# The last two row tiles of a hybrid decoder block: last tile summed in two column halves, preceding tile scaled half on GpSimd, tail in program order

## The chip, the cores and the metric

One core of a Trainium2 chip runs the whole program. The time is device microseconds of that core; it is the median of several executions. The profile is one execution recorded by the hardware profiler; its times count from the start of its span.

## The reference, cut to what matters

The program computes one decoder block on 1024 tokens of width 1024: attention and spatial gating side by side, a gated MLP with a convolution, and a final RMSNorm. The change lies in the last matrix product and in that final norm:

```python
h = h + conv_ffn(rmsnorm(h, norm_ffn_g[layer]), w_up[layer], conv_w[layer],
                 conv_b[layer], w_down[layer])
...
return rmsnorm(h, norm_final_g)        # h * rsqrt(mean(h*h) + 1e-6) * gain, row by row

def conv_ffn(x, w_up, conv_w, conv_b, w_down):
    ...
    return (jax.nn.silu(g) * a) @ w_down
```

A row of the output can be scaled only when the sum of squares over all 1024 columns of that row is known, so the norm of a row tile begins when the last part of that tile's product has been added.

## The kernel before, in words

The output is worked on in eight row tiles of 128 tokens, y0 to y7, each 128 x 1024 in SBUF. The product with `w_down` is done by Strassen's scheme (Winograd's form), in 512-wide column halves `lo` (0 to 511) and `hi` (512 to 1023): seven block products named A11, S4, A12, S1, S2, S3 and A22, each of which is computed by `dprod` for four row tiles. Each matmul with full precision is made of three float32r matmuls (high times high, high times low, low times high). The contraction runs over NP = 11 pairs of blocks, so a row tile of a block product takes 33 matmuls into one PSUM bank.

The last product is A22. Its first eight contraction steps (line 1703) go over the four row tiles in turn; the last three, the `rest`, are prepared first and then finished one row tile at a time (lines 1707 to 1710), so that bank 4 is complete first (for y4), then bank 5 (y5), 6 (y6) and 7 (y7). Nine matmuls of 512 columns lie between one tile's completion and the next. These four banks are the PSUM tiles named `s`; the other four are named `b`.

When a bank of A22 is complete, this is done for its row tile (lines 1803 to 1806 and `finish`, 1766 to 1783). By then the `hi` half is complete and already multiplied by the gain, and its squares are summed.

1. DVE subtracts the bank from the `lo` half (L1804).
2. ACT squares the `lo` half and sums the squares (L1805: an ACTIVATE and an ACTIVATION_READ_ACCUMULATOR), then takes the square root (L1770), where the other half's mean square comes in as the bias `ssb`.
3. DVE takes the reciprocal (L1771).
4. ACT scales the `hi` half (L1775) while DVE scales the `lo` half by reciprocal and gain (L1776, SCALAR_TENSOR_TENSOR).
5. SyncE's queue (SP) issues the store of the whole tile, 512 KB (L1783). For y7 step 4 runs in two pieces of 256 columns, the two `lo` quarters are stored from SP (L1779) and the `hi` half from ACT's own queue (L1781).

The order of instructions on each engine isn't the order in which they are written. The class `Pace` records all instructions of the program; `settle` works out dependences, gives each instruction a due time from the due times of those that need it, and then `run` lets a model of the engines pick, for each engine, whichever recorded instruction can start first, and of those the one due first. Two regions of the DRAM tensor `out` are compared there by their first and last address alone, so two column ranges of the same rows count as overlapping and the model lets the second store begin only when the first has landed. The order so found is fixed for each engine. Between stores to different columns the built program has no such wait: it waits only for what produces the data, and for the earlier user of the same completion semaphore, of which there are eight in rotation.

Of the kernel before, what the change touches and what calls it, by code (L numbers as in the profile page):

```python
# [11 lines left out]
AF = mybir.ActivationFunctionType  # L12
# [20 lines left out]
class Pace:  # L33
# [77 lines left out]
    def start(self):  # L111
        self.first = len(self.tc.nc.cur_bb.bb.instructions)

    def view(self, a):

        ap = getattr(a, "bass_ap", None)
        t = getattr(ap, "tensor", None)
        if t is None:
            return None
        dims = [tuple(d) for d in a.ap]  # L120
        if t.name in self.slot:
            if self.slot[t.name][0].space == "psum":
                return t.name, 0, P, 1, True
            step = 1
            for s in t.shape[1:]:
                step *= s
            p0, off = divmod(ap.offset, step)
            n = dims[0][1] if dims[0][0] else 1
            mask, run = 1, 1
            starts = [off]  # L130
            rest = sorted((d for d in dims[1:] if d[0]), reverse=True)
            if rest and rest[-1][0] == 1:
                run = rest.pop()[1]
            for s, c in rest:
                starts = [o + s * k for o in starts for k in range(c)]
            mask = 0
            for o in starts:
                mask |= ((1 << run) - 1) << o
            return t.name, p0, p0 + n, mask, True
        end = ap.offset + sum(abs(s) * (c - 1) for s, c in dims)  # L140
        return t.name, ap.offset, end + 1, 1, False
# [57 lines left out]
    def settle(self, rounds=3):  # L199

        names = {mybir.EngineType.PE: "PE", mybir.EngineType.DVE: "DVE", mybir.EngineType.Activation: "ACT",
                 mybir.EngineType.Pool: "POOL", mybir.EngineType.SP: "SP"}
        ops, seen, uses, opens = [], {}, {}, {}
        for i in list(self.tc.nc.cur_bb.bb.instructions)[self.first:]:
            eng = names.get(i.engine)
            rd = [v for v in map(self.view, i.ins) if v]
            wr = [v for v in map(self.view, i.outs) if v]
            if eng is None or not wr:
                continue
            k = len(ops)  # L210
            if eng == "PE" and not i.start_tensor_calc:
                rd = rd + wr
            deps = set()
            for w, vs in ((False, rd), (True, wr)):
                for name, a, b, m, tile_ in vs:
                    old, keep, hits = seen.setdefault(name, []), [], 0
                    for o in old:
                        hit = o[2] < b and a < o[3] and o[4] & m
                        if hit and (w or o[1] or self.bank(name) and ops[o[0]][1] != eng):
                            deps.add(o[0])  # L220
                            hits += 1
                        if not (w and hit and a <= o[2] and o[3] <= b and not o[4] & ~m and tile_):
                            keep.append(o)
                    keep.append((k, w, a, b, m))
                    seen[name] = keep
                    if tile_:
                        uses.setdefault(name, set()).add(k)
                        if not hits:
                            opens.setdefault(name, set()).add(k)
            deps.discard(k)  # L230
            c = self.cost(i, eng)
            ops.append((i, eng, c, deps, SET.get(str(getattr(i, "func", "")).split(".")[-1], 0) if eng == "ACT" else 0))
        prev = self.prior(uses)
        for name, ks in opens.items():
            for old in prev[name]:
                for k in ks:
                    ops[k][3].update(uses[old] - {k})
        whose = {}
        for name, ks in uses.items():
            whose.setdefault(self.slot[name][0], set()).update(ks)  # L240
        for p in {p: 0 for p, _ in self.slot.values()}:
            if p.after:
                ops.append((None, "TURN", (0, 0, 0), set().union(*(whose[q] for q in p.after)), 0))
                for k in whose[p]:
                    ops[k][3].add(len(ops) - 1)
        n = len(ops)
        succ = [[] for _ in range(n)]
        for k, o in enumerate(ops):
            for d in o[3]:
                succ[d].append(k)  # L250
        line, count = [k for k in range(n) if not ops[k][3]], [len(o[3]) for o in ops]
        for k in line:
            for q in succ[k]:
                count[q] -= 1
                if not count[q]:
                    line.append(q)
        assert len(line) == n, [(ops[k][0].name, str(ops[k][0])) for k in range(n) if count[k]][:4]
        at, t = [0.0] * n, 0.0
        for k, o in enumerate(ops):
            at[k] = t  # L260
            if o[1] == "PE":
                t += o[2][0]
        best = None
        for _ in range(rounds):
            due = [0.0] * n
            for k in reversed(line):
                o = ops[k]
                d = at[k] if o[1] == "PE" else at[k] + SLACK
                for s in succ[k]:
                    d = min(d, due[s] - (o[2][0] if ops[s][1] == o[1] != "SP" else o[2][1] + HOP))  # L270
                due[k] = d
            order, start, end = self.run(ops, succ, due)
            if best is None or end < best[0]:
                best = (end, order)
            at = start
        for eng, seq in best[1].items():
            for x, y in zip(seq, seq[1:]):
                self.tc.add_manual_dep(ops[y][0], ops[x][0].name, mybir.DependencyInfo(
                    mybir.DependencyClass.NoSync, mybir.DependencyReason.DATA), reason="order")
        return best[0]  # L280
# [63 lines left out]
def block_kernel(ctx: ExitStack, tc: tile.TileContext, xT, xtok, wuv, wv, wqk, wf, cpk, xg, bfv,  # L344
# [1338 lines left out]
    def dprod(xn_, wsrc, bk, first, wb=None, tail=1):  # L1683

        def prep(p_):
            xr = dt_("xr", [P, 512], F32)
            sp.dma_start(out=xr, in_=hx[p_, XI[xn_]])
            if wb is not None:
                wload(p_, wb)
            xh = dt_("xh", [P, 2, 512], F32R)  # L1690
            split_w(xr, (xh[:, 0], xh[:, 1]))
            src = wsrc(p_)
            wh = dt_("wh", [P, 2, 512], F32R)
            split_w(src, (wh[:, 0], wh[:, 1]))
            return xh, wh

        def step(m, p_, xh, wh):
            ms = slice(m * P, (m + 1) * P)
            for n, (xi, wi) in enumerate(((0, 0), (0, 1), (1, 0))):
                pe.matmul(banks[bk + m], xh[:, xi, ms], wh[:, wi, :], start=(first and p_ == 0 and n == 0),  # L1700
                          stop=(p_ == NP - 1 and n == 2), skip_group_check=True)

        for p_ in range(NP - tail):
            xh, wh = prep(p_)
            for m in range(4):
                step(m, p_, xh, wh)
        rest = [(p_, *prep(p_)) for p_ in range(NP - tail, NP)]
        for m in range(4):
            for r in rest:
                step(m, *r)  # L1710
# [55 lines left out]
    def finish(tt, done):  # L1766
# [6 lines left out]
        for c in range(0, 512, n):  # L1773
            d, t = slice(done.start + c, done.start + c + n), slice(todo.start + c, todo.start + c + n)
            act.activation(y[tt][:, d], y[tt][:, d], AF.Copy, scale=r)  # L1775
            dve.scalar_tensor_tensor(out=y[tt][:, t], in0=y[tt][:, t], scalar=r, in1=gfb[:, t],  # L1776
                                     op0=ALU.mult, op1=ALU.mult)
            if tt == 7:
                sp.dma_start(out=out[tt * P:(tt + 1) * P, t], in_=y[tt][:, t])  # L1779
        if tt == 7:  # L1780
            act.dma_start(out=out[tt * P:(tt + 1) * P, done], in_=y[tt][:, done])  # L1781
        else:
            sp.dma_start(out=out[tt * P:(tt + 1) * P, :], in_=y[tt])  # L1783

    def gain(tt, half):
        dve.tensor_tensor(out=y[tt][:, half], in0=y[tt][:, half], in1=gfb[:, half], op=ALU.mult)
# [9 lines left out]
    for m in range(4):  # L1796
# [2 lines left out]
        act.activation(x3[m], y[4 + m][:, hi], AF.Square, accum_out=ssf[:, 4 + m, 1:2])  # L1799
        first_half(4 + m, 1)  # L1800
        gain(4 + m, hi)
    dprod("A22", t4, 4, False, tail=3)
    for m in range(4):
        dve.tensor_tensor(out=y[4 + m][:, lo], in0=y[4 + m][:, lo], in1=banks[4 + m], op=ALU.subtract)  # L1804
        act.activation(x3[m], y[4 + m][:, lo], AF.Square, accum_out=ssf[:, 4 + m, 0:1])  # L1805
        finish(4 + m, hi)
    pace.settle()
    dn.release()
    upl.release()
# [47 lines left out]
```

## Time and profile before

| what | value |
|---|---|
| time, median of 3 runs | 1056.11 us (1056.04 to 1056.29) |
| time of the profiled execution | 1056.11 us |
| its span, first to last instruction | 1054.4 us |
| PE busy | 1045.7 us (99% of the span) |
| DVE busy | 914.1 us (87%) |
| ACT busy | 578.6 us (55%) |
| POOL (GpSimd) busy | 251.4 us (24%) |
| granted TensorE clock, mean | 0.999 |

The profiled execution took as long as the median run, 1.7 us more than its span; that difference lies outside the span. A row of the timeline gives start, length, engine, line, operation, output and inputs, and how many instructions are merged into it. Starts on one engine can lie closer than the lengths, since an instruction begins while the one before it still drains. A row of the table of stretches gives, for each engine, the busy time in the stretch, and at its end the granted clock, the mean busy share of the 16 DMA engines and the GB/s that they moved.

### The profile page before, as it was taken

How to read it: one execution, taken by the hardware profiler on the slowest of the kernel's cores; microseconds unless marked ns; L12 is line 12 of the kernel's file. 1: busy time of each engine (PE TensorE's matmuls, PEld its weight loads, DVE VectorE, ACT ScalarE, POOL GpSimd, SP SyncE). 2: the span in 40 equal slices, each digit the busy share in tenths (PEclk: the TensorE clock that was granted, in tenths of full speed). 3: DMA queues.
4: the chain of work that ended last, by engine and by line, in shares of the span. 5: the costliest groups of instructions: out<-in, count | busy, mean ns of one | idle time of the engine just before them, and what ended most of it. 6: DMA issues, size and time to landing. Idle time of an engine off the chain costs nothing.

```text
span 1054.4 us, 14160 instructions
## 1 busy us (share of the span) xinstructions
PE 1045.7 (99%) x4865; PEld 863.3 (82%) x4865; DVE 914.1 (87%) x1384; ACT 578.6 (55%) x1007; POOL 251.4 (24%) x212
## 2 busy tenths in 40 slices
PE   9999999999999999999999999999999999999997
PEld 6888788888888888888888888888888888888885
DVE  6996998988888869999999899999998895697774
ACT  6668555477777747645444344444444454454653
POOL 0002234233362250073432533424322000000000
PEclk9999999999999999999999999999999999999999
DMA  9243167965664454214323242332423995333352
GB/s 333 91 152 105 53 188 232 293 208 162 205 212 147 140 195 164 80 63 147 108 92 120 102 135 64 115 126 76 130 74 104 349 391 194 95 96 100 91 180 89
DMA packets 65176, 158.22 MB, mean 150 GB/s; under 512 B 7680, under 2 KB 8520, under 8 KB 65104
## 3 DMA queue, kind: packets, MB, share of 16 engines
q1 hardware_dynamic: 64672, 156.50, 45.3%
q10 hardware_dynamic: 432, 0.82, 0.3%
q8 instruction: 38, 0.62, 0.2%
q14 instruction: 34, 0.28, 0.1%
HBM read 114.98 MB, written 42.31 MB: 149 GB/s over the span
## 4 chain that ended last, share of the span: by engine, by line
PE 98%; DMA 0%; ACT 0%; DVE 0%; SPq 0%; issue 0%; ACTq 0%
PE s L1512 23%; PE b L1512 17%; PE s L1700 11%; PE b L1700 9%; PE s L551 6%; PE b L551 5%; PE fl L1183 4%; PE s L700 4%; PE po L1107 3%; PE b L700 3%; PE tr L1088 3%; PE lg L1068 2%; PE lg L1067 2%; PE b L1423 1%; PE b L1421 1%; PE b L1422 1%
## 5 line engine op out<-in xcount | busy, mean ns | idle before, releaser
L1512 PE MATMUL s<-xT,whb 128*128 128x512 f32 x804 | 189.7, 389 | 0.0
L1512 PEld LDWEIGHTS s<-xT,whb 128*128 128x128 f32 x804 | 150.7, 188 | 31.9 <-DVE whb L450 0.3
L1512 PE MATMUL b<-xB,wha 128*128 128x512 f32 x528 | 126.9, 389 | 0.0
L1700 PE MATMUL s<-whb,wha 128*128 128x512 f32 x528 | 120.2, 389 | 0.0
L1700 PEld LDWEIGHTS s<-whb,wha 128*128 128x128 f32 x528 | 99.1, 188 | 20.6
L1512 PEld LDWEIGHTS b<-xB,wha 128*128 128x128 f32 x528 | 99.0, 188 | 20.5
L444 ACT CAST whb<-sg 128x512 fp32r<-128x512 f32 x82 | 50.8, 621 | 92.9 <-PE s L1512 83.2
L444 ACT CAST wha<-sg 128x512 fp32r<-128x512 f32 x77 | 48.0, 624 | 92.4 <-PE b L1700 43.6
L1700 PE MATMUL b<-whb,wha 128*128 128x512 f32 x396 | 90.2, 389 | 0.0
L450 DVE TENSOR_TENSOR wha<-sg,wha 128x512 fp32r<-128x512 f32 x77 | 53.0, 688 | 40.1 <-ACT wha L444 40.1
L1700 PEld LDWEIGHTS b<-whb,wha 128*128 128x128 f32 x396 | 74.3, 188 | 15.4
L1401 POOL TENSOR_TENSOR sg<-raw,raw 128x512 f32<-128x512 f32 x20 | 37.3, 1864 | 159.9 <-DVE whb L450 159.9
L1512 PE MATMUL s<-xB,whb 128*128 128x512 f32 x264 | 63.5, 389 | 0.0
L1183 PE MATMUL fl<-whl,H 128*128 128x512 f32 x192 | 62.7, 406 | 0.0
L450 DVE TENSOR_TENSOR whb<-sg,whb 128x512 fp32r<-128x512 f32 x82 | 58.5, 732 | 2.5 <-ACT whb L444 2.2
L1512 PE MATMUL b<-xT,whb 128*128 128x512 f32 x252 | 60.7, 389 | 0.0
L1094 ACT CAST pt<-tr 128x512 fp32r<-128x512 f32 (+2 forms) x96 | 45.6, 476 | 24.7 <-PE tr L1088 20.9
L1099 DVE TENSOR_TENSOR pt<-tr,pt 128x512 fp32r<-128x512 f32 (+1 forms) x96 | 52.0, 551 | 7.2 <-ACT pt L1094 6.7
L1512 PEld LDWEIGHTS s<-xB,whb 128*128 128x128 f32 x264 | 49.5, 188 | 10.6 <-DVE h L1583 0.3
L1399 POOL TENSOR_TENSOR sg<-raw 128x512 f32<-128x512 f32 x20 | 41.6, 2081 | 64.5 <-DMA raw<-wup 61.3
L1512 PEld LDWEIGHTS b<-xT,whb 128*128 128x128 f32 x252 | 47.3, 188 | 9.8
L1107 PE MATMUL po<-pt,V 128*128 128x512 f32 (+1 forms) x192 | 48.5, 347 | 0.0
(373 smaller groups left out, 2287.2 us busy)
## 6 DMA issues: line engine op xcount, KB each, us to landing
raw<-wup SPq DMA_DIRECT2D x44, 512.0 KB, 3.5
sg<-hx SPq DMA_DIRECT2D x77, 256.0 KB, 2.6
hx<-hs SPq DMA_DIRECT2D x44, 256.0 KB, 4.0
hx<-ca SPq DMA_DIRECT2D x33, 256.0 KB, 2.3
xT<-wdn SPq DMA_DIRECT2D x28, 256.0 KB, 5.4
raw<-wqk SPq DMA_DIRECT2D x8, 512.0 KB, 3.7
kd<-G SPq DMA_DIRECT2D x16, 256.0 KB, 5.9
qd<-G SPq DMA_DIRECT2D x16, 256.0 KB, 3.6
```

The costliest lines, as they stand in the source:

```text
L444: act.copy(h, src)
L450: return eng.tensor_tensor(out=l, in0=src, in1=f32(h), op=ALU.subtract)
L551: pe.matmul(banks[m], xs(n, xi, k)[:, ms], w[:, wi, :], start=(first and k == 0 and c == 0), stop=(k == 3 and c == 2), skip_group_check=True)
L700: pe.matmul(ps, w[:, wi, ks], xs(n, xi, k), start=(first and c == 0), stop=(c == 11), skip_group_check=True)
L1094: act.copy(pt[:, 0, o:512], ps[:, o:512])
L1099: dve.tensor_tensor(out=pt[:, 1, o:512], in0=ps[:, o:512], in1=f32(pt[:, 0, o:512]), op=ALU.subtract)
L1107: pe.matmul(self.po[hf][:, o:512], lhs, pt[:, s, o:512], start=(k == 0 and s == 0), stop=(k == 4 * hf + 3 and s == 1), skip_group_check=True)
L1183: pe.matmul(self.bank, sgT[k][:, xi, ts_], self.w[hf, k][:, wi, :], start=(k == 0 and i == 0), stop=(k == 3 and i == 2))
L1399: pool.tensor_tensor(out=s[0], in0=a21, in1=a22, op=ALU.add)
L1401: pool.tensor_tensor(out=s[2], in0=a21, in1=a11, op=ALU.add)
L1512: pe.matmul(ps, w[:, wi, ks], xb[:, xi, k, :], start=(first and n == 0), stop=(n == 11), skip_group_check=True)
L1700: pe.matmul(banks[bk + m], xh[:, xi, ms], wh[:, wi, :], start=(first and p_ == 0 and n == 0), stop=(p_ == NP - 1 and n == 2), skip_group_c ...
```

## The change

The tail, from the last three contraction steps of A22 on, is written out instead of being looped, and `settle` is told by `plain()` where it begins: instructions of the tail get due times in the order in which they are written, and they no longer set due times of what comes ahead of them.

- **y7 in two column halves.** The last three contraction steps of y7 run for columns 0 to 255 into bank 7, then for columns 256 to 511 into bank 0 (a `b` tile, idle by then): 18 matmuls of 256 columns instead of 9 of 512. When the first nine are done, DVE subtracts the whole of bank 7 from `lo`, and ACT squares and sums columns 0 to 255. When the second nine are done, DVE subtracts columns 256 to 511 of bank 0, and ACT squares and sums those. In between a new ACT instruction (Identity, one column) adds the first quarter's mean square to `ssb`.
- **y5 and y6 scaled half on GpSimd.** For y5 and y6 GpSimd scales the `hi` half (a tensor_scalar multiply) where ACT did; y4 keeps ACT. The stores of y5 and y6 are split: the `hi` half is stored after GpSimd, the `lo` half after DVE, 256 KB each.
- **y6 behind the last subtraction.** `store(6, pool)` is written behind the last subtraction of y7, so that DVE scales y6's `lo` half after it.

```diff
@@ settle
+            if j >= self.mark:
+                tail.add(k)
...
                 d = at[k] if o[1] == "PE" else at[k] + SLACK
+                if k in tail:
+                    due[k] = 1e9 + k
+                    continue
@@ dprod
-        def step(m, p_, xh, wh):
+        def step(m, p_, xh, wh, cs=slice(0, 512), at=None):
...
-                pe.matmul(banks[bk + m], xh[:, xi, ms], wh[:, wi, :], start=(first and p_ == 0 and n == 0),
+                pe.matmul(banks[bk + m if at is None else at][:, cs], xh[:, xi, ms], wh[:, wi, cs],
+                          start=((first and p_ == 0 or at == 0 and p_ == NP - tail) and n == 0),
...
+        if tail > 1:
+            return lambda m, cs, at=None: [step(m, *r, cs, at) for r in rest]
@@ tail
-    dprod("A22", t4, 4, False, tail=3)
-    for m in range(4):
-        dve.tensor_tensor(out=y[4 + m][:, lo], in0=y[4 + m][:, lo], in1=banks[4 + m], op=ALU.subtract)
-        act.activation(x3[m], y[4 + m][:, lo], AF.Square, accum_out=ssf[:, 4 + m, 0:1])
-        finish(4 + m, hi)
+    last = dprod("A22", t4, 4, False, tail=3)
+    pace.plain()
+    def half_sum(tt, cs):
+        dve.tensor_tensor(out=y[tt][:, lo], in0=y[tt][:, lo], in1=banks[tt], op=ALU.subtract)
+        act.activation(x3[tt - 4][:, cs], y[tt][:, cs], AF.Square, accum_out=ssf[:, tt, tt // 7:tt // 7 + 1])
+    def root(tt):
+        r = ssf[:, tt, 0:1]
+        act.activation(r, r, AF.Sqrt, bias=ssb[:, tt:tt + 1], scale=1.0 / 1024)
+        dve.reciprocal(r, r)
+    def scaled(tt, cs):
+        dve.scalar_tensor_tensor(out=y[tt][:, cs], in0=y[tt][:, cs], scalar=ssf[:, tt, 0:1], in1=gfb[:, cs],
+                                 op0=ALU.mult, op1=ALU.mult)
+    def store(tt, eng):
+        r, rows = ssf[:, tt, 0:1], slice(tt * P, (tt + 1) * P)
+        if eng is act:
+            act.activation(y[tt][:, hi], y[tt][:, hi], AF.Copy, scale=r)
+            scaled(tt, lo)
+            sp.dma_start(out=out[rows, :], in_=y[tt])
+        else:
+            pool.tensor_scalar(out=y[tt][:, hi], in0=y[tt][:, hi], scalar1=r, scalar2=None, op0=ALU.mult)
+            sp.dma_start(out=out[rows, hi], in_=y[tt][:, hi])
+            scaled(tt, lo)
+            sp.dma_start(out=out[rows, lo], in_=y[tt][:, lo])
+    for tt in (4, 5, 6):
+        last(tt - 4, lo)
+        half_sum(tt, lo)
+        root(tt)
+        if tt < 6:
+            store(tt, act if tt == 4 else pool)
+    qs = [slice(c, c + 256) for c in range(0, 1024, 256)]
+    last(3, qs[0])
+    half_sum(7, qs[0])
+    last(3, qs[1], 0)
+    dve.tensor_tensor(out=y[7][:, qs[1]], in0=y[7][:, qs[1]], in1=banks[0][:, qs[1]], op=ALU.subtract)
+    act.activation(ssb[:, 7:8], ssf[:, 7, 1:2], AF.Identity, bias=ssb[:, 7:8], scale=1.0 / 1024)
+    act.activation(x3[3][:, qs[1]], y[7][:, qs[1]], AF.Square, accum_out=ssf[:, 7, 0:1])
+    store(6, pool)
+    root(7)
+    r = ssf[:, 7, 0:1]
+    for c in range(2):
+        act.activation(y[7][:, qs[2 + c]], y[7][:, qs[2 + c]], AF.Copy, scale=r)
+        scaled(7, qs[c])
+        sp.dma_start(out=out[7 * P:8 * P, qs[c]], in_=y[7][:, qs[c]])
+    act.dma_start(out=out[7 * P:8 * P, hi], in_=y[7][:, hi])
```

The end of DVE's order before (`s` are the banks of A22, `gms` holds the sums of squares, `gfb` the gain):

```order
L1771 RECIPROCAL gms_996<-gms_996 128x1
L1776 SCALAR_TENSOR_TENSOR y5_8302<-y5_8302,gms_996,gfb_7809 128x512
L1771 RECIPROCAL gms_996<-gms_996 128x1
L1776 SCALAR_TENSOR_TENSOR y6_8304<-y6_8304,gms_996,gfb_7809 128x512
L1804 TENSOR_TENSOR y7_8306<-y7_8306,s_1357_7817 128x512
L1771 RECIPROCAL gms_996<-gms_996 128x1
L1776 SCALAR_TENSOR_TENSOR y7_8306<-y7_8306,gms_996,gfb_7809 128x256 x2
```

And in the changed kernel (`b_1350` is bank 0):

```order
L1825 SCALAR_TENSOR_TENSOR y5_8302<-y5_8302,gms_996,gfb_7809 128x512
L1814 TENSOR_TENSOR y7_8306<-y7_8306,s_1357_7817 128x512
L1821 RECIPROCAL gms_996<-gms_996 128x1
L1851 TENSOR_TENSOR y7_8306<-y7_8306,b_1350_7810 128x256
L1825 SCALAR_TENSOR_TENSOR y6_8304<-y6_8304,gms_996,gfb_7809 128x512
L1821 RECIPROCAL gms_996<-gms_996 128x1
L1825 SCALAR_TENSOR_TENSOR y7_8306<-y7_8306,gms_996,gfb_7809 128x256 x2
```

The subtraction of y7 has become two, and the scaling of y6 moved from ahead of it to behind both.

The end of SyncE's queue before:

```order
L1687 DMA sg_1593_9517<-hx_116 128x512
L1783 DMA out<-y4_8300 128x1024
L1783 DMA out<-y5_8302 128x1024
L1783 DMA out<-y6_8304 128x1024
L1779 DMA out<-y7_8306 128x256 x2
```

And in the changed kernel, where L1837 stores a `hi` half, L1839 a `lo` half and L1860 a quarter of y7:

```order
L1834 DMA out<-y4_8300 128x1024
L1837 DMA out<-y5_8302 128x512
L1837 DMA out<-y6_8304 128x512
L1860 DMA out<-y7_8306 128x256
L1839 DMA out<-y5_8302 128x512
L1839 DMA out<-y6_8304 128x512
L1860 DMA out<-y7_8306 128x256
```

The `lo` halves of y5 and y6 stand behind the first quarter of y7, and the second quarter of y7 behind them. On ACT's queue the store of y7's `hi` half stays last. Ahead of the tail one pair of rows changes places: DVE splits the weights of the ninth contraction step (`whb_9505`) after two gain multiplications instead of before them.

More of the change, by code (lines that the diff above doesn't have):

```diff
@@ L112, in start, with plain @@
         self.first = len(self.tc.nc.cur_bb.bb.instructions)
+    def plain(self):
+        self.mark = len(self.tc.nc.cur_bb.bb.instructions)
     def view(self, a):
@@ L203, in settle @@
         ops, seen, uses, opens = [], {}, {}, {}
-        for i in list(self.tc.nc.cur_bb.bb.instructions)[self.first:]:
+        tail = set()
+        for j, i in list(enumerate(self.tc.nc.cur_bb.bb.instructions))[self.first:]:
             eng = names.get(i.engine)
@@ L1777, in finish @@
                                      op0=ALU.mult, op1=ALU.mult)
[L1778 to L1783, printed above, removed]
+        sp.dma_start(out=out[tt * P:(tt + 1) * P, :], in_=y[tt])
     def gain(tt, half):
```

## The prediction

> **What bounds the kernel now.** I read the page's chain first, to see where a change can pay at all.
>
> ```profile
> span 1054.4 us, 14160 instructions
> PE 98%; DMA 0%; ACT 0%; DVE 0%; SPq 0%; issue 0%; ACTq 0%
> ```
>
> TensorE carries the chain for 98% of the span, and the change leaves TensorE's work alone except for its last nine matmuls. So everything is decided in the last microseconds. Second, the chain piece by piece over those (start, length, what), and the timeline for TensorE's last stretch and the last stores:
>
> ```profile
> 1034.82 10.44 PE s L1700 x46
> ...
> 1045.28 0.70 DVE y L1804
> ...
> 1046.00 0.73 ACT xB L1805 x2
> ...
> 1046.76 0.30 ACT gms L1770
> ...
> 1047.09 0.17 DVE gms L1771
> ...
> 1047.29 0.75 DVE y L1776
> 1048.04 0.61 DVE y L1804
> ...
> 1048.67 0.73 ACT xB L1805 x2
> ...
> 1049.43 0.30 ACT gms L1770
> ...
> 1049.76 0.18 DVE gms L1771
> ...
> 1049.95 0.91 ACT y L1775 x2
> ```
>
> ```profile
> 1039.19 8.10 PE L1700 MATMUL s<-whb,wha 128*128 128x512 f32 x35
> 1050.47 0.83 SPq L1779 DMA_DIRECT2D out<-y  x2
> 1050.89 0.40 ACTq L1781 DMA_DIRECT2D out<-y  x1
> ```
>
> TensorE ends at 1039.19 + 8.10 = 1047.29, but the chain leaves it at 1045.26, when y6's bank is complete: y6 goes through subtraction, squares, root, reciprocal and its scaling on DVE (1047.29), and only then does DVE subtract y7's bank (pipelined start 1047.96). y7 thus waits 0.67 us for DVE. Then squares, root, reciprocal, scaling, and the stores are issued between 1050.47 and 1051.30. The remaining 3.1 us to 1054.40 are transfers and their end. Third, therefore, the stretches (last two numbers: busy share of the DMA engines, GB/s), with the issue of y4's store for the delay between issue and data:
>
> ```profile
> 1044.04 0.34 SPq L1783 DMA_DIRECT2D out<-y  x1
> ```
>
> ```profile
> 1044.40:1044.80 0.40, 0.40 (x3) 0.35 (x2) 0.16 (x1) 0.21 (x1) 0.00 (x0) 1.00 0.00 0
> 1044.80:1045.20 0.40, 0.40 (x3) 0.32 (x3) 0.00 (x0) 0.40 (x2) 0.00 (x0) 1.00 0.85 338
> 1048.40:1051.20 2.80, 0.00 (x0) 0.00 (x0) 1.29 (x4) 1.92 (x5) 0.00 (x0) 1.00 0.95 375
> 1051.20:1051.60 0.40, 0.00 (x0) 0.00 (x0) 0.00 (x0) 0.00 (x0) 0.00 (x0) 0.80 0.67 218
> 1051.60:1052.80 1.20, 0.00 (x0) 0.00 (x0) 0.00 (x0) 0.00 (x0) 0.00 (x0) 0.50 0.95 335
> 1052.80:1053.20 0.40, 0.00 (x0) 0.00 (x0) 0.00 (x0) 0.00 (x0) 0.00 (x0) 0.50 0.28 87
> 1053.20:1054.40 1.20, 0.00 (x0) 0.00 (x0) 0.00 (x0) 0.00 (x0) 0.00 (x0) 0.50 0.00 0
> ```
>
> Data begin about 0.82 us after an issue starts (0.85 of the second stretch is busy, so from 1044.86). The stretch to 1051.20 moves 2.80 x 375 = 1,050 KB, which is y5 and y6; the three behind it move 87 + 402 + 35 = 524 KB, which is y7. The last byte leaves at 1052.8 + 35/335 = 1052.90, and 1.50 us later the span ends. The transfer engines are 95% busy in both large stretches: the tail has a second limit, bytes, hard behind the chain.
>
> **The change, part by part.** Rows for the pieces, before the sums:
>
> ```profile
> 1045.89 0.15 DVE L1771 RECIPROCAL gms<-gms 128x1 f32<-128x1 f32 x1
> 1046.08 0.75 DVE L1776 SCALAR_TENSOR_TENSOR y<-y,gms,gfb 128x512 f32<-128x512 f32 x1
> 1046.76 0.29 ACT L1770 ACTIVATE gms<-gms 128x1 f32<-128x1 f32 x1
> 1046.96 1.32 ACT L1775 ACTIVATE y<-y,gms 128x512 f32<-128x512 f32 x2
> L1099 DVE TENSOR_TENSOR pt<-tr,pt 128x256 fp32r<-128x256 f32 x16 | 6.7, 416 | 0.0
> L1094 ACT CAST pt<-tr 128x256 fp32r<-128x256 f32 x16 | 5.8, 365 | 4.2 <-PE lg L1067 2.5 <-PE tr L1088 1.0 <-PE lg L1068 0.6
> L1775 ACT ACTIVATE y<-y,gms 128x256 f32<-128x256 f32 x2 | 0.9, 500 | 0.2 <-DVE gms L1771 0.2
> ```
>
> *TensorE.* 18 matmuls of 256 columns replace 9 of 512. 512 columns are (8.10 - 0.39) / 34 = 0.227 us apart. No row has 256 in a series; 384 columns are 0.18 apart, and four of 128 columns, each with weights of its own, (0.60 - 0.27) / 3 = 0.11:
>
> ```profile
> 228.20 0.34 PE L1067 MATMUL lg<-x 128*128 128x384 f32 x1
> 228.38 0.34 PE L1068 MATMUL lg<-x,x 128*128 128x384 f32 x1
> 230.45 0.60 PE L1088 MATMUL tr<-ident,G 128*128 128x128 f32 x4
> ```
>
> So 256 lie between 0.11 and 0.18; following the step from 512 to 384 I take 0.13: 18 x 0.13 = 2.34 against 9 x 0.227 = 2.04, 0.3 us more. Halves are complete near 1046.35 and 1047.5.
>
> *DVE.* y5's scaling starts at 1046.08 as before, the next instruction 0.67 later. y7's first subtraction takes that place at 1046.75 (its data have been ready for 0.4 us), y6's reciprocal follows 0.61 later at 1047.36, the second subtraction 0.19 behind that at 1047.55 (TensorE is ready at 1047.5), and by L1099's 0.42 us it ends at 1047.97. Before, the only subtraction ended near 1048.65. y6's scaling then runs until about 1048.65, under ACT's work.
>
> *ACT.* y7's first squares (256 columns; 0.365 to 0.50, I take 0.42) and their sum run from 1047.45 to 1047.97, and the new Identity starts at 1048.0. The next instruction can start 0.20 later, as L1775 does behind L1770, so Identity costs 0.2 us: second squares at 1048.20. They and their sum take 0.73 - 0.21 = 0.52; the root begins at 1048.75, the reciprocal at 1049.08 and the scaling at 1049.27 instead of 1049.95. **The chain to the scaling is 0.68 us shorter**: 0.67 of DVE's wait and 0.21 of the squares gained, 0.2 lost again. No table load stands in the tail of ACT's order, before or after, so none is counted.
>
> *The stores.* y7's first quarter can be issued at 1050.47 - 0.68 = 1049.79 and the `hi` half from ACT at 1050.21. But on SP's queue two stores that were ready long before, the `lo` halves of y5 (done 1046.8) and y6 (1048.7), now stand behind that first quarter, and SP issues in order. At 0.34 us each they go out at 1050.13 and 1050.47, and the last quarter at 1050.81, against 1050.90 before: of 0.68 us the last issue keeps 0.1. And the bytes behind the first quarter have doubled: 1,049 KB (512 KB of y7, 256 KB each of y5 and y6) against 524.
>
> First data at 1049.79 + 0.82 = 1050.61. The first 0.4 us carry one small store alone, 87 KB as in the row at 1051.20. 962 KB are left, at 335 GB/s (y7's short rows) to 375 (whole tiles): 2.57 to 2.87 us, so the last byte leaves at 1053.58 to 1053.88, I take 1053.7, against 1052.90. If the first 0.4 us are full too it is 1053.4. **Sum: 0.8 us later**, with bounds +0.5 and +1.0.
>
> *GpSimd.* Its multiplies are of a kind that no row shows.
>
> ```profile
> L1139 POOL CAST A<-t 128x512 fp32r<-128x512 f32 x4 | 2.5, 614 | 0.2
> 260.02 0.61 POOL L1139 CAST A<-t 128x512 fp32r<-128x512 f32 x1
> L1399 POOL TENSOR_TENSOR sg<-raw 128x512 f32<-128x512 f32 x20 | 41.6, 2081 | 64.5 <-DMA raw<-wup 61.3 <-DVE whb L450 2.5 <-ACT whb L444 0.7
> 798.58 1.29 POOL L1402 TENSOR_TENSOR sg<-sg,raw 128x512 f32<-128x512 f32 x1 [2.50 <-DVE whb L450]
> ```
>
> Bounds are 0.61 (a copy) and 2.08 (two inputs beside a busy DVE); nearest is the copy, one tensor in and one out, and I take 0.7. y5's runs from 1046.1, y6's from 1047.55 to 1048.25; both stores are issued before 1048.7 and their bytes are through by 1050.3. Cover ends at 1049.79, when y7's first quarter wants the queue. The copies that leave ACT (1.32 us) weren't on the chain.
>
> *DVE's weights* for the ninth step now come about 1.4 us later than here:
>
> ```profile
> 1026.91 0.69 DVE L450 TENSOR_TENSOR whb<-xT,whb 128x512 fp32r<-128x512 f32 x1
> ```
>
> TensorE first needs them at 1039.19, so this costs nothing.
>
> **The forecast** is 1056.11 (the profiled execution, which equals the median) + 0.8 = 1056.9 us. Changes within 0.2%, 2.1 us, count as no change here.
>
> **Rivals.**
>
> *The bytes don't queue* and the last issue sets the end: 1050.81 against 1050.90, so 0.1 us is gained, 1056.0; if the early halves slip through beside y7 and only ACT's last store counts, 0.68, 1055.4. For it: SP has idle time between 1048.7 and 1049.8, and the transfers are spread over 16 engines. Against it: a busy share of 0.95 with only half these bytes. The Trainium skill ("DMA: Bandwidth & Descriptors", section "Anatomy of one DMA — SWDGE (gpsimd) path") fits each DMA as a fixed 2.0 us and bytes over 436 GB/s; taken alone, the last 128 KB would land 2.3 us after issue, and the end would move with that issue, as in this rival. The rows of this trace bear a slower rate and a queue out.
>
> *GpSimd is late and holds SP's queue* (slower). Its two multiplies stand ahead of y7's first quarter on SP. From 1046.1, they decide when together they pass 3.7 us (1049.79). At 2.08 each y6's `hi` half goes out at 1050.3 and joins the burst: from 1051.0, 1,311 KB at 355 GB/s end at 1054.7, +1.8, 1057.9; each further us adds one, so beyond 4.5 us together it is slower by over 0.2%. For it: L1399's mean, and GpSimd idle since 799.9. Against it: this kernel's first copy on GpSimd (260.02) took 0.61 like the later ones. The Trainium skill ("GPSIMD Engine Reference", section "2.1 Instruction dispatch") says that the first call of a freshly loaded kernel pays about 6 us more; the end would then be near 1061. No run here shows such a first call.
>
> *TensorE's halves cost 0.18 each*: 3.24 us for 18, the second half complete at 1048.4 instead of 1047.5. DVE then waits for it and scales y6 later; the chain's 0.68 is gone, and the doubled burst ends 1.5 to 1.7 us later than before: 1057.7. Against it: a half must cost less than 384 columns.
>
> **How the numbers follow.** Forecast 0.70 (1056.5 to 1057.2), bytes that don't queue 0.16 (1055.4 to 1056.3), GpSimd late 0.10 (1057.5 up), slow halves 0.04 (1057.7). The range from 1055.5 to 1058.0 takes in the first two and the lower part of the others, with room for unsharp terms. Faster by over 0.2% would need 2.1 us where the chain yields 0.68: 0.03. Slower by over 0.2% is the upper half of the late GpSimd and a rest: 0.07. Within 0.2%: 0.90.
>
> **What would show it.** Right: the subtraction of y7 starts near 1046.75, y7's scaling near 1049.3, four issues on SP follow each other from 1049.8 without a pause, and the DMA engines stay over 90% busy from 1051 to 1053.6. Wrong: a GpSimd multiply over 1.7 us, SP's first quarter of y7 issued after 1050.2, idle stretches between the last transfers, or a last byte before 1053.0.

## The result and the profile after

| what | before | changed |
|---|---|---|
| time, median of 22 runs each | 1056.22 us (1055.78 to 1057.35) | 1058.16 us (1056.90 to 1059.32) |
| ratio, 95% interval | | 1.0018 (1.0012 to 1.0024) |
| profiled execution, its span | 1056.11, 1054.4 us | 1058.28, 1056.5 us |

The change costs 1.94 us. That lies within the 0.2% called no change (the interval reaches just beyond it), but it is more than twice the 0.8 us that the prediction summed, and the time lies outside its range (1055.5 to 1058.0). Nearest to it is the rival with the late GpSimd, 1057.9 us.

The page of the changed kernel (its head, and GpSimd's group of the tail: busy time, mean ns of one, idle time ahead of it), and then the chain piece by piece (start, length, what), show TensorE at 98% as before, and a shorter way from y6's bank to y7's scaling.

```profile
span 1056.5 us, 14186 instructions
PE 98%; DMA 1%; ACT 0%; DVE 0%; SPq 0%; issue 0%; ACTq 0%
...
L1836 POOL TENSOR_SCALAR y<-y,gms 128x512 f32<-128x512 f32 x2 | 3.9, 1956 | 246.1 <-DVE gms L1821 246.1
```

```profile
1034.95 10.67 PE s L1709 x47
...
1045.65 0.69 DVE y L1814
...
1046.44 0.75 DVE y L1825
1047.19 0.61 DVE y L1814
...
1049.62 0.91 ACT y L1858 x2
```

The tails of profiles must be laid on each other at a common point, for they don't start alike: over the kernels told of here, the subtraction of y4, ahead of everything that differs, starts between 1040.87 and 1042.77 us after the span's start, 1041.20 before the change. Here it starts at 1041.57. From there to y7's scaling it is 1049.62 - 1041.57 = 8.05 us, against 1049.95 - 1041.20 = 8.75: the chain is 0.70 us shorter. To the end of the span it is 14.93 us against 13.20: 1.73 longer. (The medians differ by 1.94; a single profile doesn't tell 0.2 us from chance.) So 2.4 us were lost behind the scaling. The timeline of the changed kernel, engine by engine, shows where:

```profile
1041.57 0.69 DVE L1814 TENSOR_TENSOR y<-y,s 128x512 f32<-128x512 f32 x1 [3.41 <-PE s L1709]
...
1046.52 1.24 PE L1709 MATMUL b<-whb,wha 128*128 128x256 f32 x9
...
1046.51 3.90 POOL L1836 TENSOR_SCALAR y<-y,gms 128x512 f32<-128x512 f32 x2 [246.07 <-DVE gms L1821]
...
1050.44 0.33 SPq L1837 DMA_DIRECT2D out<-y  x1
1050.81 0.43 SPq L1860 DMA_DIRECT2D out<-y  x1
1051.29 1.29 SPq L1839 DMA_DIRECT2D out<-y  x2
1052.68 0.54 SPq L1860 DMA_DIRECT2D out<-y  x1
...
1050.55 0.41 ACTq L1861 DMA_DIRECT2D out<-y  x1
```

GpSimd's two multiplies take 3.90 us together, to 1050.41. Only then can SP issue y6's `hi` half (1050.44), and behind it y7's first quarter (1050.81). That is the 1,956 ns for one in the page's row, and SP's waits for it (total, times, longest) say the same:

```profile
SPq L1837 <- POOL y L1836: 5.3, 2, 3.9
```

Last, the stretches (granted clock, busy share of the DMA engines and GB/s at the end of each row):

```profile
1050.40:1051.20 0.80, 0.00 (x0) 0.00 (x0) 0.10 (x1) 0.12 (x1) 0.01 (x1) 0.50 0.00 0
1051.20:1054.80 3.60, 0.00 (x0) 0.00 (x0) 0.00 (x0) 0.00 (x0) 0.00 (x0) 0.50 1.00 362
1054.80:1056.40 1.60, 0.00 (x0) 0.00 (x0) 0.00 (x0) 0.00 (x0) 0.00 (x0) 0.50 0.02 5
```

For 0.8 us nothing is transferred, and then everything is left: 3.60 x 362 + 1.60 x 5 = 1,311 KB, that is y7 (524), the `lo` halves of y5 and y6 (524) and y6's `hi` half (262). The engines are full (share 1.00) until the last byte at about 1054.83, which is 13.26 us behind y4's subtraction, against 1052.90 - 1041.20 = 11.70 before.

### The profile page after: what moved, and what is told of

It is laid out like the page before. It is cut to its first block, busy times and chain, and to the rows that moved or that the text cites. A ratio compares the mean times of both kernels' runs of the same rounds, so it can differ in the third digit from the quotient of the medians.

```text
span 1056.5 us, 14186 instructions
## 1 busy us (share of the span) xinstructions
PE 1046.0 (99%) x4874; PEld 864.3 (82%) x4874; DVE 915.1 (87%) x1385; ACT 576.7 (55%) x1008; POOL 254.1 (24%) x214
## 4 chain that ended last, share of the span: by engine, by line
PE 98%; DMA 1%; ACT 0%; DVE 0%; SPq 0%; issue 0%; ACTq 0%
PE s L1521 23%; PE b L1521 17%; PE s L1709 11%; PE b L1709 8%; PE s L560 6%; PE b L560 5%; PE fl L1192 4%; PE s L709 4%; PE po L1116 3%; PE b L709 3%; PE tr L1097 3%; PE lg L1077 2%; PE lg L1076 2%; PE b L1432 1%; PE b L1430 1%; PE b L1431 1%
## 5 line engine op out<-in xcount | busy, mean ns | idle before, releaser
L1709 PE MATMUL s<-whb,wha 128*128 128x512 f32 (+1 forms) x528 | 119.2, 387 | 0.0
L1709 PE MATMUL b<-whb,wha 128*128 128x512 f32 (+1 forms) x405 | 91.5, 387 | 0.0
L1836 POOL TENSOR_SCALAR y<-y,gms 128x512 f32<-128x512 f32 x2 | 3.9, 1956 | 246.1 <-DVE gms L1821 246.1
```

Source lines behind the costliest of these rows:

```text
L1709: pe.matmul(banks[bk + m if at is None else at][:, cs], xh[:, xi, ms], wh[:, wi, cs], start=((first and p_ == 0 or at == 0 and p_ == NP - ...
```

## The experiments

Each is the changed kernel with the edit shown. The last two columns are from the profiled execution of each, counted from the start of y4's subtraction: to the start of y7's scaling, and to the end of the span. Single profiled executions lie up to 1.3 us from the median of their kernel, largely because they reach the tail earlier or later; the two columns leave that out.

| kernel | median, and of before run beside it | difference | ratio, 95% | to y7's scaling | to the end |
|---|---|---|---|---|---|
| before | 1056.22 | | | 8.75 | 13.20 |
| changed | 1058.16, 1056.22 | +1.94 | 1.0018 (1.0012 to 1.0024) | 8.05 | 14.93 |
| no multiplies | 1055.64, 1056.37 | -0.73 | 0.9994 (0.9985 to 1.0002) | 8.05 | 12.56 |
| no multiplies, same order | 1057.32, 1056.37 | +0.95 | 1.0010 (1.0001 to 1.0019) | 8.05 | 14.13 |
| `lo` halves first | 1056.93, 1056.37 | +0.56 | 1.0005 (0.9996 to 1.0014) | 8.06 | 13.67 |
| y6's `hi` half last | 1056.76, 1056.49 | +0.27 | 1.0001 (0.9992 to 1.0010) | 8.05 | 13.33 |
| y6's multiply twice | 1059.19, 1056.49 | +2.70 | 1.0023 (1.0014 to 1.0033) | 8.05 | 15.93 |
| nothing on GpSimd | 1056.18, 1056.49 | -0.31 | 0.9997 (0.9988 to 1.0006) | 8.12 | 12.63 |
| and the addition on DVE | 1055.92, 1056.50 | -0.58 | 0.9994 (0.9985 to 1.0003) | 8.19 | 12.77 |

Where the interval holds 1, the kernel is not told apart from the one before. Only three intervals lie clear of 1, all above it: those of the changed kernel, of the same order without multiplies, and of y6's multiply twice.

The next to last column hardly moves: the 0.70 us of the chain are there in all of them, or 0.56 at the least. All the rest is what happens to the stores.

### No multiplies on GpSimd

The `hi` halves of y5 and y6 are stored unscaled. Without the multiplies the planner also finds another order for SP: all four half stores go ahead of y7's.

```diff
-            pool.tensor_scalar(out=y[tt][:, hi], in0=y[tt][:, hi], scalar1=r, scalar2=None, op0=ALU.mult)
```

> The two GpSimd multiplies are left out, so the hi halves of y5 and y6 are stored unscaled (this part of the computation is missing); the planner then puts all four of their stores ahead of y7's first quarter. Theory 1 (the loss is GpSimd's length plus the order of the stores on SP): with both gone the chain's 0.68 us comes through, only y7's 524 KB are left in the last burst, 0.6 us faster than the kernel before. Theory 3 (the column halves or the split stores cost time themselves): no faster than before, 0 to +1.9 us.

Measured: 0.73 us faster than before, by an interval that still holds 1. The timeline (L1838 stores a `lo` half, L1859 a quarter of y7) shows both `lo` halves gone before y7's quarters, and y7's first quarter issued 1050.70 - 1042.14 = 8.56 us behind y4's subtraction, against 1050.47 - 1041.20 = 9.27 before the change:

```profile
1042.14 0.69 DVE L1814 TENSOR_TENSOR y<-y,s 128x512 f32<-128x512 f32 x1 [3.41 <-PE s L1709]
...
1047.80 2.12 SPq L1838 DMA_DIRECT2D out<-y  x2
1050.70 0.81 SPq L1859 DMA_DIRECT2D out<-y  x2
```

The two `hi` halves, which now wait for nothing in the tail, were issued long before it, at 1027.36 and 1028.62. With these stores out of the way nearly all of the chain's gain reaches the end: 0.64 of 0.70 us in the profile. But this run changed two things, the multiplies and SP's order; the next keeps the order.

### The same, with SP's order of the changed kernel

```diff
+        sp_ = [k for k in best[1]["SP"] if k in tail]
+        best[1]["SP"] = [k for k in best[1]["SP"] if k not in tail] + [sorted(sp_)[j] for j in (0, 1, 3, 5, 2, 4, 6)]
```

> As the kernel without the multiplies (hi halves of y5 and y6 unscaled), but SP's stores in the changed kernel's order, lo halves of y5 and y6 behind y7's first quarter. Theory 1: what the prediction summed without a late GpSimd, +0.8 us against the kernel before (two thirds of the loss is GpSimd: 1.1 of 1.9 us). Theory 2 (the store order and the doubled bytes alone make the loss, GpSimd's length is hidden): +1.9 us, as the changed kernel. If the order costs nothing: -0.6 us, as the kernel with the lo halves ahead.

Measured: 0.95 us slower than before. In the timeline (L1838 stores a `hi` half, L1840 a `lo` half, L1861 a quarter of y7):

```profile
1041.97 0.69 DVE L1816 TENSOR_TENSOR y<-y,s 128x512 f32<-128x512 f32 x1 [3.41 <-PE s L1711]
...
1050.54 0.33 SPq L1861 DMA_DIRECT2D out<-y  x1
1050.91 0.93 SPq L1840 DMA_DIRECT2D out<-y  x2
1051.94 0.79 SPq L1861 DMA_DIRECT2D out<-y  x1
```

This is the changed kernel as the prediction imagined it, with GpSimd out of the way: y7's first quarter goes out 8.57 us behind y4's subtraction, 0.70 earlier than before, and 1,049 KB follow. The forecast said +0.8, the run says +0.95. Between this run and the one ahead of it only SP's order differs, and it is worth 0.95 + 0.73 = 1.7 us. (Here the `hi` halves leave behind y4's store and not 17 us earlier, but that isn't what costs: the transfer engines have nothing to do from 1049 until y7's first data.) Between this run and the changed kernel only GpSimd's multiplies differ: 1.94 - 0.95 = 1.0 us (0.80 by the two profiles). That agrees with the burst: it starts with y6's `hi` half issued at 1050.44 - 1041.57 = 8.87 us instead of y7's quarter at 8.57, 0.30 later, and holds 262 KB more, at 362 GB/s 0.72 us; together 1.02.

### `lo` halves first on SP

The changed kernel with its multiplies, and SP's order y5 `lo`, y5 `hi`, y6 `lo`, y6 `hi`, then y7.

```diff
+        best[1]["SP"] = [k for k in best[1]["SP"] if k not in tail] + [sorted(sp_)[j] for j in (0, 2, 1, 4, 3, 5, 6)]
```

> The changed kernel whole, only SP's order of the last stores differs: y5 lo, y5 hi, y6 lo, y6 hi, then both quarters of y7. Theory 1: y7's first quarter still waits for the second multiply (near 1050.4 in the changed kernel's profile), but the burst behind it is 786 KB instead of 1311, so about 1.4 us less than the changed kernel: +0.5 us against the kernel before. Theory 2: the whole loss goes, 0 or below. If only GpSimd's length counts and bytes don't: +1.5 to +1.9 us.

Measured: 0.56 us slower than before, 1.38 less than the changed kernel loses. (L1839 stores a `hi` half, L1862 a quarter of y7.)

```profile
1042.53 0.69 DVE L1816 TENSOR_TENSOR y<-y,s 128x512 f32<-128x512 f32 x1 [3.41 <-PE s L1711]
...
1051.40 0.33 SPq L1839 DMA_DIRECT2D out<-y  x1
1051.83 1.24 SPq L1862 DMA_DIRECT2D out<-y  x2
```

y7's first quarter is as late as in the changed kernel: it goes out 1051.83 - 1042.53 = 9.30 us behind y4's subtraction, there 1050.81 - 1041.57 = 9.24, so GpSimd still holds the queue. What is gone is the 524 KB of the two `lo` halves from the last burst: at the 362 GB/s of the changed kernel's stretch 1.45 us, against 1.38 by the medians and 1.26 by the profiles.

### y6's `hi` half last on SP

```diff
+        best[1]["SP"] = [k for k in best[1]["SP"] if k not in tail] + [sorted(sp_)[j] for j in (0, 2, 1, 4, 5, 6, 3)]
```

> The changed kernel whole, only SP's order differs: y5 lo, y5 hi, y6 lo, both quarters of y7, and y6's hi half, which waits for GpSimd's second multiply, last. Theory 1 (GpSimd's second multiply holds back what stands behind it): y7's first quarter goes out 0.6 us earlier than in the changed kernel, the last burst has 786 KB from about then, and the time falls below that of the order with y6's hi half ahead of y7 (+0.56 us measured), to between -0.3 and +0.2 us against the kernel before. If only the bytes of the burst count: the same +0.5 us as with y6's hi half ahead.

Measured: 0.27 us slower than before, not told apart from it, and just above the range expected. (L1862 stores a quarter of y7, L1839 a `hi` half.)

```profile
1040.87 0.69 DVE L1816 TENSOR_TENSOR y<-y,s 128x512 f32<-128x512 f32 x1 [3.41 <-PE s L1711]
...
1049.43 0.82 SPq L1862 DMA_DIRECT2D out<-y  x2
1050.35 0.45 SPq L1839 DMA_DIRECT2D out<-y  x1
```

Now nobody stands behind GpSimd: y7's first quarter goes out at 8.56, as without multiplies. The last burst is the same 786 KB as in the run ahead of it (y7 and y6's `hi` half). There it begins with the `hi` half, issued 1051.40 - 1042.53 = 8.87 us behind y4's subtraction, here 0.31 earlier; the end comes 0.29 (medians) to 0.34 us (profiles) earlier. With GpSimd's multiplies as they are, SP's order alone thus takes back 1.7 of the 1.9 us.

### y6's multiply twice

GpSimd multiplies y6's `hi` half first into a scratch tile and then in place. SP's order is kept.

```diff
+            if tt == 6:
+                prb = dn.tile([P, 512], F32, name="prb")
+                pool.tensor_scalar(out=prb, in0=y[tt][:, hi], scalar1=r, scalar2=None, op0=ALU.mult)
```

> The changed kernel with SP's order kept and y6's multiply on GpSimd done twice (once to a scratch tile first), so that its hi half comes one multiply, 1.95 us, later. Theory 1: everything behind it on SP moves by 1.95 us; only the store of y7's hi half from ACT's queue fills the gap, so 262 KB leave the burst and the end moves by about 1.3 us: +3.2 us against the kernel before. The prediction's rival said one us for each further us: +3.9 us. If GpSimd isn't on the path: +1.9 us as the changed kernel.

Measured: 2.70 us slower than before, 0.76 beyond the changed kernel (1.00 by the profiles). Rows of the timeline (L1842 stores a `hi` half, L1866 y7's `hi` half):

```profile
1042.77 0.69 DVE L1816 TENSOR_TENSOR y<-y,s 128x512 f32<-128x512 f32 x1 [3.41 <-PE s L1711]
...
1047.71 2.12 POOL L1841 TENSOR_SCALAR y<-y,gms 128x512 f32<-128x512 f32 x1 [246.35 <-DVE gms L1823]
1049.82 1.79 POOL L1840 TENSOR_SCALAR prb<-y,gms 128x512 f32<-128x512 f32 x1
1051.70 1.56 POOL L1841 TENSOR_SCALAR y<-y,gms 128x512 f32<-128x512 f32 x1
...
1053.29 0.33 SPq L1842 DMA_DIRECT2D out<-y  x1
...
1051.75 0.40 ACTq L1866 DMA_DIRECT2D out<-y  x1
```

SP issues y6's `hi` half at 1053.29 - 1042.77 = 10.52 us instead of 8.87, so 1.65 later; the end moves by less. The stretches show why:

```profile
1052.40:1053.20 0.80, 0.00 (x0) 0.00 (x0) 0.00 (x0) 0.00 (x0) 0.80 (x1) 0.50 0.69 261
1053.20:1054.00 0.80, 0.00 (x0) 0.00 (x0) 0.00 (x0) 0.00 (x0) 0.06 (x1) 0.50 0.18 67
```

While SP waits, y7's `hi` half goes out from ACT's own queue: 0.8 x 261 + 0.8 x 67 = 262 KB, which at 362 GB/s takes 0.72 us out of the last burst. 1.65 - 0.72 = 0.93. Here a delay of SP's queue cost its length less what the other queue moved in the meantime. The +3.2 us expected were too many, in part because the added multiply was counted at 1.95 us: y6's `hi` half comes only 1.65 later, for the last two of the three take 1.79 and 1.56. The run also shows GpSimd's length directly on the path.

### Nothing on GpSimd

All work is done: y5's `hi` half on ACT, y6's on DVE, and the planner compares column ranges of `out` exactly, so that it puts the half stores ahead of y7's.

```diff
-        return t.name, ap.offset, end + 1, 1, False
+        return t.name + ("@%d" % (ap.offset % 1024) if t.name == "out" else ""), ap.offset, end + 1, 1, False
...
-            pool.tensor_scalar(out=y[tt][:, hi], in0=y[tt][:, hi], scalar1=r, scalar2=None, op0=ALU.mult)
+            if tt == 5:
+                act.activation(y[tt][:, hi], y[tt][:, hi], AF.Copy, scale=r)
+            else:
+                dve.tensor_scalar(out=y[tt][:, hi], in0=y[tt][:, hi], scalar1=r, scalar2=None, op0=ALU.mult)
```

> All of the work, nothing on GpSimd: the column halves of y7 and y6's scaling behind the last subtraction stay, y5's hi half is scaled on ACT, y6's hi half on DVE, and the planner compares column ranges of the output exactly, so all four half stores go out ahead of y7. Theory 1: near the kernel that left the multiplies out (-0.73 us measured), less what the two scalings cost on ACT and DVE: -0.6 to -0.2 us against the kernel before. Theory 3 (GpSimd is of use for shortening ACT's or DVE's part): 0 or above.

Measured: 0.31 us faster than before by the medians, 0.57 by the profiles; the interval of the ratio holds 1. Against the changed kernel it is 2.2 us. The stores are split as in the changed kernel, so splitting them isn't what costs in the changed kernel. DVE does in 0.49 us what takes GpSimd four times as long:

```profile
1048.94 0.49 DVE L1839 TENSOR_SCALAR y<-y,gms 128x512 f32<-128x512 f32 x1
```

### And the mean-square addition on DVE

```diff
-    act.activation(ssb[:, 7:8], ssf[:, 7, 1:2], AF.Identity, bias=ssb[:, 7:8], scale=1.0 / 1024)
+    dve.scalar_tensor_tensor(out=ssb[:, 7:8], in0=ssf[:, 7, 1:2], scalar=1.0 / 1024, in1=ssb[:, 7:8], op0=ALU.mult, op1=ALU.add)
```

> Nothing on GpSimd: y5's right half is scaled on ScalarE and y6's on VectorE, as in the run before this one, and besides the mean-square of y7's second half is added to the first one's on VectorE instead of ScalarE. Theory (the early stores are out of the way, and the end goes with the chain to y7's scaling): the run before this one gained 0.31 us on the kernel before; the addition on VectorE saves one start of ScalarE of some 0.2 us on that chain, and the end comes earlier by the same: 0.4 to 0.6 us under the kernel before. Rival (the last bytes queue behind the other stores): what the chain saves is lost again in the queue, and it stays at 0.3 us under the kernel before.

Measured: 0.58 us faster than before, an interval that still holds 1, and one that can't be told from the run ahead of it. The number is the one expected, but not by the step expected, which isn't there: y7's scaling starts 8.19 us behind y4's subtraction, not earlier than the 8.12 of the run ahead. Rows of DVE and ACT say why:

```profile
1041.83 0.69 DVE L1814 TENSOR_TENSOR y<-y,s 128x512 f32<-128x512 f32 x1 [3.41 <-PE s L1709]
...
1048.70 0.49 DVE L1839 TENSOR_SCALAR y<-y,gms 128x512 f32<-128x512 f32 x1
1049.10 0.15 DVE L1856 SCALAR_TENSOR_TENSOR gms<-gms 128x1 f32<-128x1 f32 x1
1049.17 0.74 DVE L1825 SCALAR_TENSOR_TENSOR y<-y,gms,gfb 128x512 f32<-128x512 f32 x1
1049.83 0.15 DVE L1821 RECIPROCAL gms<-gms 128x1 f32<-128x1 f32 x1
...
1049.35 0.29 ACT L1820 ACTIVATE gms<-gms 128x1 f32<-128x1 f32 x1 [0.22 <-DVE gms L1856]
```

The addition stands behind y6's multiply on DVE, ACT's root waits 0.22 us for it and starts at 1049.35 - 1041.83 = 7.52, where it was 7.53 in the run ahead; the reciprocal then waits for y6's scaling. The start that ACT saves comes back as a wait for DVE. Where the 0.3 us between the medians of these two runs come from isn't shown; their intervals overlap almost wholly. Both are clearly faster than the changed kernel, and neither is shown to be faster than the one before.

### What a GpSimd multiply takes by itself

Two kernels with extra GpSimd operations on scratch tiles ahead of the tail; only their profiles are used. In the first the operations run beside the work of DVE and ACT:

> The changed kernel with seven more GpSimd operations on scratch tiles before the tail, for their lengths alone: a copy, a multiply by a constant, multiplies by a per-row scalar of 128, 256 and 512 columns, a two-input multiply with the scalar spread over the columns, and a two-input multiply. Theory 1a (the per-row scalar makes the length): copy and constant near 0.6 to 0.8 us, per-row scalar 1.9 us at 512 columns and in proportion below. Theory 1b (the multiply slows beside a busy DVE or ACT in the tail): the per-row scalar takes 0.6 to 1.0 us where DVE is idle. Time as the changed kernel.

```profile
1023.56 2.27 POOL L1812 COPY prb<-y 128x512 f32<-128x512 f32 x1 [223.96 <-DVE gms L1750]
1025.93 1.49 POOL L1813 TENSOR_SCALAR prc<-prb 128x512 f32<-128x512 f32 x1
1027.52 1.06 POOL L1815 TENSOR_SCALAR prb<-prc,gms 128x256 f32<-128x256 f32 x1
1028.56 0.60 POOL L1814 TENSOR_SCALAR prb<-prc,gms 128x128 f32<-128x128 f32 x1
1029.26 2.16 POOL L1816 TENSOR_SCALAR prb<-prc,gms 128x512 f32<-128x512 f32 x1
1031.50 1.04 POOL L1817 TENSOR_TENSOR prc<-prb,gms 128x512 f32<-128x512 f32 x1
```

In the second they run while DVE and ACT have nothing to do:

> The changed kernel with three GpSimd operations on scratch tiles between DVE's last split and the tail, where DVE and ACT do nothing: a multiply by a per-row scalar of 512 columns, a copy of 512, a multiply by a constant of 256. Theory 1a (the multiply is as long by itself): 1.9 to 2.0 us for the first, with the copy at 0.6. Theory 1b (DVE's reads beside it make it long, as the first probe's copy of 2.27 us beside a busy DVE suggests): 0.6 to 1.0 us for the first.

```profile
1038.72 1.57 POOL L1815 TENSOR_SCALAR prb<-wha,gms 128x512 f32<-128x512 f32 x1 [237.98 <-DVE wha L459]
1040.35 0.61 POOL L1816 COPY prc<-prb 128x512 f32<-128x512 f32 x1
1041.05 0.85 POOL L1817 TENSOR_SCALAR prb<-prc 128x256 f32<-128x256 f32 x1
```

Undisturbed, the multiply takes 1.57 us where a copy of the same size takes 0.61. The scalar from a tile isn't the reason: with a constant, half the columns take 0.85, which is about as much per column, and 512 columns took 1.49 in the first kernel. Beside the other engines' work both are longer, and the length goes with the columns (0.60, 1.06, 2.16 for 128, 256, 512). The tail's 1.95 lies between, and in the run with y6's multiply twice the three instances fall from 2.12 over 1.79 to 1.56 as DVE and ACT run out of work. The form of the operation counts too: the same product written as a multiply of two tensors, the second being the scalar spread over the columns (L1817), took 1.04 us, and DVE worked during 0.60 us of that time. It wasn't tried in the tail.

## Why the prediction was wrong

The step that failed is one term of the sum: the duration of GpSimd's multiply, "nearest is the copy, one tensor in and one out, and I take 0.7". It takes 1.95 us in the tail and 1.57 alone. The bounds held (0.61 and 2.08), but the value was taken at the wrong end: a tensor in and a tensor out don't make an operation a copy. Nor does the length alone decide. By the prediction's own times, two multiplies of 1.57 would end near 1046.1 + 3.14 = 1049.24, still ahead of the 1049.79 at which y7's first quarter wants the queue (an estimate; no run has such multiplies in the tail). It took the work of DVE and ACT beside them as well. With 3.90 us for two, the threshold of 3.7 which the prediction gave for its rival was passed, and the outcome was the rival: SP's queue held, 1,311 KB in one burst, "+1.8, 1057.9" against +1.94 and 1058.16. That rival got a chance of 0.10 because of the same misjudged row, and the range held only its lower part. Of the 1.14 us between forecast and measurement (1.94 - 0.8) the multiplies make 1.0 by the medians (1.94 - 0.95) and 0.80 by the profiles; the rest is a term for the order and the bytes that was a little small.

Step by step:

- *TensorE's halves.* Right. 0.13 us apart were taken; nine take 1.24 us, and by the way the prediction counts, (1.24 - 0.27) / 8 = 0.12.
- *DVE and ACT.* Right. 0.68 us were forecast for the chain, 0.70 came, in every run that keeps these steps.
- *SP's order and the bytes.* Right in mechanism, a little small. Without the multiplies the same order gave +0.95 against +0.8. The burst starts 0.70 us earlier than before and holds 524 KB more, at 362 GB/s 1.45 us: +0.75. The two kernels without multiplies (-0.73 and +0.95) show that this order alone is worth 1.7 us. The issues were forecast at 0.34 us each and the last quarter 0.1 us earlier than before; they became longer, and in the same-order run without multiplies it was issued at 1051.94 - 1041.97 = 9.97 us, against about 1050.90 - 1041.20 = 9.70 before. Since the transfer engines were full by then, the bytes set the end and not this issue.
- *"The bytes don't queue."* Fell: nothing on GpSimd's side delays the same-order run, and it is slower all the same, by an interval that lies above 1. (The fit that the prediction set beside this rival is one for transfers that GpSimd issues; here SP and ACT issue them.)
- *"Each further us adds one."* Too simple. A delay of 1.65 us cost 0.76 to 1.00, since y7's `hi` half used the time from ACT's queue.
- *A first call on GpSimd.* The Trainium skill ("GPSIMD Engine Reference", section "2.1 Instruction dispatch") was cited with some 6 us more for the first call of a freshly loaded kernel. No row here shows it: after 246 us of idle time GpSimd's first multiply started with its data, and two took 3.90 us together.

Of the signs of being wrong, two came true: a multiply over 1.7 us, and y7's first quarter issued after 1050.2 (1050.81, or 1050.44 if the later start of this profile, 0.37 us, is taken off). A third, idle time between the last transfers, came in part: 0.8 us ahead of the burst and none in it. The signs of the chain came true as well: with 0.37 taken off, y7's subtraction starts at 1046.74 and its scaling at 1049.25.

## What to carry to other kernels

Before a store is placed in a queue, ask for each entry when its data are ready in the worst case; a slow producer holds every ready store behind it, and here the order of seven stores was worth 1.7 us, more than the 0.70 that the shorter chain gained. Bytes that are ready early should leave early, because the last burst runs at the full rate of the transfer engines and each 262 KB in it cost 0.7 us. An operation that the trace doesn't show should be tried beside the work that it will meet, or both ends of its bounds belong in the range, when one end lies beyond the point from which it decides. Here the middle of the bounds (1.35 us) and even the time by itself (1.57) lay below that point, 1.85 us for each of two.

## What the runs showed of the hardware

- GpSimd beside the other engines. A copy of 128 x 512 took 0.61 us with DVE and ACT idle and 2.27 beside their work. In the other direction, DVE's split of the weights, which took 0.69 us before the change, took 1.16 and 1.77 beside GpSimd's operations with two inputs:

```profile
1031.93 1.16 DVE L459 TENSOR_TENSOR wha<-sg,wha 128x512 fp32r<-128x512 f32 x1 [0.85 <-ACT wha L453]
1033.01 1.77 DVE L459 TENSOR_TENSOR whb<-xT,whb 128x512 fp32r<-128x512 f32 x1
```

  The Trainium skill ("GPSIMD Engine Reference", section "1. Specifications") says that the two share their SBUF interfaces and contend when a DVE instruction has two SBUF inputs, as these have; the rows agree, though ACT worked too and was not tried apart. Which side loses time differs from row to row. Beside GpSimd's multiplies with one input, the same split kept its 0.68 us, and DVE's multiplication by the gain, also with two inputs, took 0.81 to 1.03 instead of 0.68. In the tail GpSimd alone lost: y6's scaling on DVE (two inputs in SBUF) took 0.75 us beside the multiplies and 0.74 without them, and DVE's subtraction, which has one input in PSUM, 0.68 as before the change.
- The same page (section "3.1 Elementwise — side-by-side cycle accounting") gives 768 ns for 512 elements as the best case of a GpSimd loop. The copy came below it (0.61), the multiply took twice as much (1.57).
- SP's issue of a store took 0.33 us by itself and 0.38 to 0.45 soon behind another one: in the changed kernel 0.43 at 1050.81, while nothing was transferred yet. Further back in the row it became longer still, 0.81 for the first of the next two and 0.54 for the last in the changed kernel, 0.79 for the last in the same-order run without multiplies; but with y6's multiply twice none of five took over 0.46. What lengthens it wasn't tried.
